# Folding the tokens of the Fourier group ahead of the DFT, and its channel products in three products of parts

## The chip, the core and the metric

The kernel runs on one core of a Trainium2 chip. The metric is the time of one execution on the device, in microseconds; lower is better. TensorE (PE in the profile) multiplies and writes to PSUM, VectorE (DVE), ScalarE (ACT) and GpSimd (POOL) do the elementwise work, and DMAs are issued by SyncE (SP), ScalarE and GpSimd.

## The reference

One layer of an encoder block on 256 tokens of width 2048, in float32: a normalised input is projected to q, k, v and u; twelve attention heads work on q, k, v; a Fourier group of four channel groups of 128 works on u; both results are normalised, joined, projected and added to x; a gated feed-forward part and a last normalisation follow. The part that changes is the Fourier group:

```python
def _fourier_mix(u, w_fourier):
    B, S = u.shape[0], u.shape[1]
    ug = u.reshape(B, S, N_FOURIER_GROUPS, FOURIER_GROUP_DIM).astype(jnp.float32)
    f = jnp.real(jnp.fft.fft2(ug, axes=(1, 3), norm='ortho'))
    y = jnp.einsum('bsgc,gcd->bsgd', f.astype(u.dtype), w_fourier)
    return y.reshape(B, S, FOURIER_WIDTH)
```

The real part of the two-dimensional DFT is cos over positions times cos over channels, less sin over positions times sin over channels. Position k and position 256-k have the same cosine and opposite sines, so the kernel computes the products for 129 cosines and 127 sines only and joins them into 256 positions at the end.

## The kernel before

Products of float32 matrices are done by parts: each operand is split into a high part, rounded to the matmul's reduced float32 (F32R), and a low part, the rest; high x high, low x high and high x low are summed in PSUM. The weights come in *units* of 1 MB (`raw`, three buffers). ScalarE rounds a unit to its high part, VectorE subtracts to get the low part, two units ahead of the multiplication; when the low part is done, the load of the unit three further on is issued on SyncE's queue.

The order is written by hand. `unit(i, work)` runs what was posted under `before` for unit i, then the unit's matmuls, then what was posted `beside` it, then the split of unit i+2, then what was posted `behind` it. Every engine takes its instructions in that order, so a step's place sets both its due time and what queues behind it. Units 0 to 3 give u (in PSUM tiles `ps_u`), 4 to 7 give v (`ps_v`), 8 to 23 the k and q heads, 24 to 39 the output projection; then come the feed-forward items. The numbers of raw tiles are unit numbers: raw7 is the weights of unit 7.

The Fourier group is done in steps posted between these units:

- `rows_out` (L462): u, scaled by each token's 1/rms (`r1`, from GpSimd), leaves PSUM as `u_hi` (L466, ScalarE) and `u_lo` (L467, VectorE), beside unit 5; both blocks of 128 tokens.
- `fourier_positions` (L529): the constant `pos` (cosines and sines of the positions, two blocks of 128 tokens x 256 columns) is split into `pos_hi` and `pos_lo`, beside unit 5.
- `fourier_weights` (L540) before unit 6: the channel DFT is multiplied into `w_fourier`, giving `ps_g` for cosine and sine; `fourier_weights_out` (L550) copies them to `Gs` in plain float32.
- `fourier_rows` (L559) before unit 7: for each of four groups six F32R matmuls (two token blocks x three products), with u as the weights and 256 columns of `pos` moving, into `ps_f`. `fourier_rows_out` (L571) copies the result to `uf` in plain float32, alternately on ScalarE and VectorE.
- `fourier_channels` (L582), before units 8, 9, 10 and 11, one group each: two plain F32 matmuls, 129 columns of cosine and 127 of sine, into `ps_y`. `fourier_channels_copy` brings the result to SBUF, `fourier_channels_join` adds and subtracts to get the 256 positions, `fourier_channels_out` squares and splits it for the output projection.

`row_by_hbm` (L318), behind unit 4, writes the token scales `r1` to HBM as a row by a GpSimd DMA, and reads them back over all partitions (`r1b`) for the keys.

PSUM tiles come from two pools of four banks: `mm` holds u, v, k, q; `dn` holds the Fourier and attention products.

Of the kernel before, what the change touches and what calls it, by code (L numbers as in the profile page):

```python
# [13 lines left out]
P = 128  # L14
D = 2048
S = 256
# [13 lines left out]
WARM = 7  # L30

U_HEAD, U_ROW = 16, 768


SHIFT = 16
# [83 lines left out]
def block_kernel(  # L119
# [30 lines left out]
    def bank(pool, name):  # L150
        return pool.tile([P, 512], F32, tag=pool.name, name=name)
# [66 lines left out]
    vec = base.tile([P, 232], F32, tag="vec", name="vec")  # L218
    chan = cat_pool.tile([P, 512], F32, tag="cat", name="chan")[:, 0 : 2 * P]
    wfs = cat_pool.tile([P, FW], F32, tag="cat", name="wfs")  # L220
    pos = cat_pool.tile([P, 2, S], F32, tag="cat", name="pos")
    Gs = [cat_pool.tile([P, FW], F32, tag="cat", name=f"G{c}") for c in range(2)]
    pos_hi = cat_pool.tile([P, 2, S], F32R, tag="cat", name="pos_hi")
    pos_lo = cat_pool.tile([P, 2, S], F32R, tag="cat", name="pos_lo")
    chan_parts = cat_pool.tile([P, 2, 2 * P], F32R, tag="cat", name="chan_parts")
    wfs_parts = [cat_pool.tile([P, FW], F32R, tag="cat", name=f"wfs_{p}") for p in ("hi", "lo")]
    rel = cat_pool.tile([P, 512], F32, tag="cat", name="rel")
# [156 lines left out]
    def at(when, i, f, *a):  # L384
        when.setdefault(i, []).append((f, a))
# [85 lines left out]
    def row_parts(name):  # L471
        return [
            ph.tile([P, 2, FW], F32R, tag=f"{name}_{p}", name=f"{name}_{p}")
            for p in ("hi", "lo")
        ]

    u_hi, u_lo = row_parts("u")
    v_hi, v_lo = row_parts("v")
    r1b = ph.tile([P, S], F32, tag="r1b", name="r1b")
    for c in range(2, 4):  # L480
        at(beside, 4, token_sums, c)
    at(beside, 4, lambda: fourier_parts())
    at(beside, 4, token_scales)
    at(beside, 5, rows_out, u_hi, u_lo, ps_u)
    at(behind, 5, query_scales)

    cat = {}

# [60 lines left out]

    def fourier_weights_out():  # L550
        for part in range(2):
            nc.scalar.activation(Gs[part], held.pop(("g", part)), AF.Copy)

    H = S // 2
    us = []

    def fourier_rows():  # L559
        for g in range(NG):  # L560
            ps = held["f", g] = bank(dn, f"ps_f{g}")
            for b in range(2):
                for n, (u, w) in enumerate(
                    [(u_hi, pos_hi), (u_hi, pos_lo), (u_lo, pos_hi)]
                ):
                    nc.tensor.matmul(
                        ps[:, 0:S], u[:, b, g * P : (g + 1) * P], w[:, b, :],
                        start=b == 0 and n == 0, stop=b == 1 and n == 2,
                    )

    def fourier_rows_out():  # L571
        for g in range(NG):
            t = ph.tile([P, 512], F32, tag="sc", name=f"uf{g}", bufs=4)[:, 0:S]
            if g % 2:
                nc.scalar.activation(t, held.pop(("f", g))[:, 0:S], AF.Copy)
            else:
                nc.vector.tensor_copy(t, held.pop(("f", g))[:, 0:S])
            us.append(t)

    sq_f = ph.tile([P, S], F32, tag="sqf", name="sq_f")  # L580

    def fourier_channels(g):  # L582
        ps = held["y", g] = bank(dn, f"ps_y{g}")
        for part, o, n in ((0, 0, H + 1), (1, H + 1, H - 1)):
            nc.tensor.matmul(
                ps[:, o : o + n], Gs[part][:, g * P : (g + 1) * P],
                us[g][:, o : o + n], start=True, stop=True,
            )


    def fourier_channels_copy(g):
        h = held["h", g] = ph.tile([P, S], F32, tag="tmp", name=f"yh{g}", bufs=2)
        nc.scalar.activation(h, held.pop(("y", g))[:, 0:S], AF.Copy)

    def fourier_channels_join(g):
        h = held.pop(("h", g))
        y = held["y", g] = ph.tile([P, S], F32, tag="add", name=f"y{g}", bufs=2)
        nc.vector.tensor_tensor(y[:, 1:H], h[:, 1:H], h[:, H + 1 : S], ALU.add)
        nc.vector.tensor_tensor(
            y[:, H + 1 : S], h[:, H - 1 : 0 : -1], h[:, S - 1 : H : -1], ALU.subtract  # L600
        )
        nc.vector.tensor_copy(y[:, 0 : H + 1 : H], h[:, 0 : H + 1 : H])

    def fourier_channels_out(g):
        feature_out(held.pop(("y", g)), NH + g, vcol(V_GF + g), sq_f, g == 0)
# [12 lines left out]
    at(before, 6, fourier_weights)  # L618
    at(beside, 6, fourier_weights_out)
    at(behind, 4, row_by_hbm, r1, r1b, "1")  # L620
    at(before, 7, fourier_rows)
    at(beside, 7, fourier_rows_out)
    at(beside, 8, lambda: rows_out(v_hi, v_lo, ps_v))
    at(behind, 8, distances)

    def fourier_channels_steps():
        for g in range(NG):
            i = 8 + g
            at(before, i, fourier_channels, g)
            at(beside, i, fourier_channels_copy, g)  # L630
            at(behind, i, fourier_channels_join, g)
            at(beside, i + 1, fourier_channels_out, g)
        at(behind, N_OUT + 1, total_scale, sq_f, "f", FW)
# [752 lines left out]
def _layout(inp):  # L1386

    import numpy as np

    f = lambda a: np.ascontiguousarray(np.asarray(a), dtype=np.float32)  # L1390
    x = f(inp["x"]).reshape(2, P, D)

    def tiles(v):
        return f(v).reshape(-1, P).T

    def moving(w, cols):

# [24 lines left out]
    w_up = np.asarray(inp["w_up"])  # L1422
    wup = np.concatenate(
        [still(w_up, o + j * P) for j in range(NF) for o in (0, DFF)]
    )
    w_dn = np.asarray(inp["w_down"])
    def rows_by(tiles, cols):

        w = f(w_dn[tiles[0] * P : (tiles[-1] + 1) * P, cols : cols + 512])
        return w.reshape(len(tiles), P, 512).transpose(1, 0, 2).reshape(P, -1)  # L1430

    downs = [
        rows_by(range(k, k + m), c + n)
        for first, m in GROUPS
        for c in (0, 512)
        for k in (first, first + m)
        for n in (0, 1024)
    ]
    late = [rows_by(LATE, 512 * c) for c in range(4)]
    dw = f(inp["dw_w"]).reshape(3, NF, P).transpose(2, 1, 0).reshape(P, 3 * NF)  # L1440
    sink = np.broadcast_to(f(inp["sink"])[None, :], (P, NH))
    vecs = np.concatenate(
        [tiles(inp["norm2_g"]), tiles(inp["attn_out_g"]),
         tiles(inp["fourier_out_g"]), dw, tiles(inp["dw_b"]), sink], axis=1,
    )
    t = np.arange(S)
    ang = 2.0 * np.pi * ((t[:, None] * t[None, :]) % S) / S
    c_pos = np.concatenate(
        [np.cos(ang[:, : S // 2 + 1]), np.sin(ang[:, 1 : S // 2])], axis=1
    )  # L1450
    c_pos = c_pos.reshape(2, P, S).transpose(1, 0, 2)
    k = np.arange(P)
    ang = 2.0 * np.pi * ((k[:, None] * k[None, :]) % P) / P
    c_chan = np.concatenate([np.cos(ang), -np.sin(ang)], axis=1) / np.sqrt(S * P)
    dist = np.abs(t[:, None] - t[None, :]).astype(np.float64)
    c_rel = np.where(dist <= WINDOW, dist, FAR).reshape(2, P, S).transpose(1, 0, 2)
    return {
        "x": np.ascontiguousarray(x.transpose(1, 0, 2)),
        "w_u_x": np.ascontiguousarray(u_x),
        "vecs": np.ascontiguousarray(vecs),  # L1460
        "wf": np.ascontiguousarray(f(inp["w_fourier"]).transpose(1, 0, 2).reshape(P, FW)),
        "w_in": win,
        "w_out": wout,
        "w_up": wup,
        "w_down_two": np.stack(downs[:8]),
        "w_down": np.stack(downs[8:]),
        "w_down_late": np.stack(late),
        "w_down_last": np.stack([rows_by(LAST, 512 * c) for c in range(4)]),
        "normf_g": f(inp["normf_g"]),
        "c_pos": np.ascontiguousarray(c_pos, dtype=np.float32),  # L1470
        "c_chan": np.ascontiguousarray(c_chan, dtype=np.float32),
        "c_rel": np.ascontiguousarray(c_rel.reshape(P, 2 * S), dtype=np.float32),
    }
# [16 lines left out]
```

## Time and profile before

| | |
|---|---|
| median of 3 runs | 934.08 us (933.99 to 934.61) |
| the profiled execution | 934.68 us |
| its span, first to last instruction | 932.9 us |
| granted TensorE clock | 0.997 |
| PE, VectorE, ScalarE busy | 99%, 83%, 58% |
| position DFT `ps_f`, 24 matmuls | 45.21 to 48.09 us in the chain |
| channel products `ps_y`, four times | 53.52, 59.43, 65.35 and 71.97 us |

The views used are: the page (busy times and the chain of work that ended last), the chain in order of time (start, length, matmul), the timeline of one engine (start, length, engine, line, operation, out<-in, and in brackets the idle time before it and what ended it), the rows of one tile, DMA issues with their time to landing, and the stretches (busy time of each engine in a stretch, granted clock, DMA share and GB/s). A matmul's own duration in a timeline includes its pipeline; its price in a stream is the distance to the next one, which the chain shows. An instruction `LDWEIGHTS` (PEld) is the load of a matmul's weights.

### The profile page before, as it was taken

How to read it: one execution, taken by the hardware profiler on the slowest of the kernel's cores; microseconds unless marked ns; L12 is line 12 of the kernel's file. 1: busy time of each engine (PE TensorE's matmuls, PEld its weight loads, DVE VectorE, ACT ScalarE, POOL GpSimd, SP SyncE). 2: the span in 40 equal slices, each digit the busy share in tenths (PEclk: the TensorE clock that was granted, in tenths of full speed). 3: DMA queues.
4: the chain of work that ended last, by engine and by line, in shares of the span. 5: the costliest groups of instructions: out<-in, count | busy, mean ns of one | idle time of the engine just before them, and what ended most of it. 6: DMA issues, size and time to landing. Idle time of an engine off the chain costs nothing.

```text
span 932.9 us, 12860 instructions
## 1 busy us (share of the span) xinstructions
PE 924.0 (99%) x4981; PEld 800.8 (86%) x4981; DVE 772.4 (83%) x988; ACT 542.3 (58%) x675; POOL 63.0 (7%) x80
## 2 busy tenths in 40 slices
PE   9999999999999999999999999999999999999996
PEld 7888998888888888888888888888888888888885
DVE  7668988787768877898878997888979789989995
ACT  7756776546455655566555665555755556655553
POOL 0101111200000000000000000000000000000002
PEclk9999999999999999999999999999999999999998
DMA  9965877657778668788798779887787968779652
GB/s 365 316 216 169 248 237 209 209 180 276 229 264 275 201 200 261 242 276 261 230 288 256 239 212 299 224 261 234 264 243 241 309 221 271 238 234 272 204 180 91
DMA packets 59309, 224.96 MB, mean 241 GB/s; under 512 B 24400, under 2 KB 29904, under 8 KB 35696
## 3 DMA queue, kind: packets, MB, share of 16 engines
q1 hardware_dynamic: 54560, 194.39, 58.3%
q0 software_dynamic: 4544, 29.49, 17.1%
q8 instruction: 39, 0.64, 0.3%
q10 hardware_dynamic: 144, 0.26, 0.1%
q14 instruction: 22, 0.18, 0.1%
HBM read 217.04 MB, written 7.08 MB: 240 GB/s over the span
## 4 chain that ended last, share of the span: by engine, by line
PE 98%; DMA 0%; ACT 0%; DVE 0%; issue 0%; POOLq 0%; POOL 0%; ACTq 0%
PE ps_val L364 25%; PE ps_gate L364 25%; PE ps_q L364 7%; PE ps_P L1161 3%; PE ps_P L1160 3%; PE ps_P L1162 3%; PE ps_N L1160 3%; PE ps_N L1161 3%; PE ps_N L1162 3%; PE ps_a L347 2%; PE ps_k L364 2%; PE ps_a L349 2%; PE ps_a L348 2%; PE ps_s L676 1%; PE ps_o L770 1%; PE ps_ff L347 1%
## 5 line engine op out<-in xcount | busy, mean ns | idle before, releaser
L203 DVE TENSOR_TENSOR lo<-raw,hi 128x2048 fp32r<-128x2048 f32 (+2 forms) x133 | 294.9, 2220 | 31.9 <-ACT hi L195 31.5
L195 ACT ACTIVATE hi<-raw 128x2048 fp32r<-128x2048 f32 (+1 forms) x131 | 246.8, 1886 | 28.2 <-PE ps_a L348 10.2
L364 PE MATMUL ps_gate<-hU,hi 128*128 128x512 f32 x688 | 236.2, 389 | 0.0
L364 PE MATMUL ps_val<-hU,hi 128*128 128x512 f32 x688 | 236.2, 389 | 0.0
L364 PE MATMUL ps_gate<-hU,lo 128*128 128x256 f32 x688 | 190.0, 276 | 0.0
L364 PE MATMUL ps_val<-hU,lo 128*128 128x256 f32 x687 | 189.7, 276 | 0.0
L364 PEld LDWEIGHTS ps_val<-hU,hi 128*128 128x128 f32 x688 | 129.2, 188 | 26.9
L364 PEld LDWEIGHTS ps_gate<-hU,hi 128*128 128x128 f32 x688 | 129.1, 188 | 26.8
L364 PEld LDWEIGHTS ps_gate<-hU,lo 128*128 128x128 f32 x688 | 129.2, 188 | 1.3
L364 PEld LDWEIGHTS ps_val<-hU,lo 128*128 128x128 f32 x687 | 129.0, 188 | 1.3
L941 ACT ACTIVATE ft_g<-ps_gate 128x256 f32<-128x256 f32 x43 | 16.5, 384 | 120.6 <-PE ps_gate L364 120.6
L941 ACT ACTIVATE ft_v<-ps_val 128x256 f32<-128x256 f32 x43 | 16.4, 383 | 86.7 <-PE ps_val L364 86.7
L364 PE MATMUL ps_q<-hT,hi 128*128 128x512 f32 x192 | 65.0, 391 | 0.0
L1160 PE MATMUL ps_P<-hi_P,op_P 128*128 128x512 f32 x144 | 56.1, 389 | 0.0
L1161 PE MATMUL ps_P<-hi_P,op_P 128*128 128x512 f32 x144 | 56.0, 389 | 0.0
L1162 PE MATMUL ps_P<-lo_P,op_P 128*128 128x512 f32 x144 | 56.0, 389 | 0.0
L364 PE MATMUL ps_q<-hT,lo 128*128 128x256 f32 x192 | 51.3, 277 | 0.0
L1058 DVE TENSOR_TENSOR lo_N<-sumw,hi_N 128x2048 fp32r<-128x2048 f32 (+1 forms) x20 | 41.5, 2076 | 9.4 <-ACT hi_N L1057 9.2
L1160 PE MATMUL ps_N<-hi_N,op_N 128*128 128x512 f32 x108 | 42.0, 389 | 0.0
L1161 PE MATMUL ps_N<-hi_N,op_N 128*128 128x512 f32 x108 | 42.0, 389 | 0.0
L1162 PE MATMUL ps_N<-lo_N,op_N 128*128 128x512 f32 x108 | 42.0, 389 | 0.0
L364 PEld LDWEIGHTS ps_q<-hT,hi 128*128 128x128 f32 x192 | 35.2, 188 | 6.6
(402 smaller groups left out, 1588.8 us busy)
## 6 DMA issues: line engine op xcount, KB each, us to landing
raw<-in_w_up SPq DMA_DIRECT2D x86, 1024.0 KB, 6.8
raw<-in_w_in SPq DMA_DIRECT2D x20, 1024.0 KB, 7.2
raw<-in_w_out SPq DMA_DIRECT2D x16, 1024.0 KB, 5.0
sumw<-in_w_down POOLq DMA_DIRECT2D x16, 1024.0 KB, 8.6
raw<-in_w_down_late SPq DMA_DIRECT2D x4, 1024.0 KB, 6.9
raw<-in_w_down_last SPq DMA_DIRECT2D x4, 768.0 KB, 4.3
turnp<-flip SPq DMA_DIRECT2D x44, 64.0 KB, 1.9
flop<-turnp SPq DMA_DIRECT2D x11, 256.0 KB, 3.2
```

Source lines behind the costliest of these rows:

```text
L195: nc.scalar.activation(halves[i][0][:, s], raws[i][:, s], AF.Copy)
L203: nc.vector.tensor_tensor(lo[:, s], raws[i][:, s], f32(hi[:, s]), ALU.subtract)
L347: nc.tensor.matmul(ps, ah, wh, start=first and q == q0, stop=False)
L348: nc.tensor.matmul(ps, al, wh, start=False, stop=False)
L349: nc.tensor.matmul(ps, ah, wl, start=False, stop=last and q == q0 + len(kk) - 1)
L364: nc.tensor.matmul(ps[:, x], (hi, lo)[i][:, k * P : (k + 1) * P], hk(k)[:, x], start=n == 0 and k == 0, stop=n == len(order) - 1 and k == ...
L676: nc.tensor.matmul(ps[:, b * S : (b + 1) * S], qT[:, qo + b * P : qo + (b + 1) * P], kT[:, ko : ko + S], start=n == 0, stop=n == 2,)
L941: nc.scalar.activation(tmp, ps[:, S : 2 * S], AF.Copy)
L1058: nc.vector.tensor_tensor(lo, src, f32(hi), ALU.subtract)
L1160: nc.tensor.matmul(ps, o[:, 0, p, :], hi[:, s], start=first and p == 0, stop=False)
L1161: nc.tensor.matmul(ps, o[:, 1, p, :], hi[:, s], start=False, stop=False)
L1162: nc.tensor.matmul(ps, o[:, 0, p, :], lo[:, s], start=False, stop=last and p == n - 1)
```

## The change

Tokens t and 256-t, for t from 1 to 127, have the same cosine and opposite sines, so their sum and their difference are formed once and the DFT over positions runs over 128 rows instead of 256. Token 0 stays as it is; token 128 is put beside it, in row 0, and the constants of row 0 are set to fit.

- `fold_turned`, `fold_back`, `fold` and `fold_low` take the place of `rows_out` for u. Tokens 128 to 255 are scaled to SBUF on ScalarE and turned by two VectorE transposes, the second of which reads reversed, so that the 32 rows of each quadrant stand in reverse order. Five DMAs on ScalarE's queue put the quadrants in reverse order at the partitions 1 to 127 and token 128 at partition 0. VectorE forms sum and difference with tokens 0 to 127, ScalarE rounds them, VectorE takes the low parts.
- `fourier_rows` now runs before unit 8. For each group three products with the difference and three with the sum, of 260, 130, 194 and three times 130 columns: sines at columns 0 to 129 of the PSUM tile, cosines at 130 to 259.
- `fourier_rows_out` splits the result into F32R parts (`uf_hi`, `uf_lo`), and `fourier_weights_out` splits `Gs` likewise. `fourier_channels`, before units 9 to 12, is three products of parts for sine and three for cosine, 130 columns each.
- `fourier_channels_copy` copies the sine half only; `fourier_channels_join` reads the cosine half from PSUM. The cosines stand with odd positions first, then even ones.
- The constant `pos` has 402 columns instead of 512.

```diff
     u_hi, u_lo = row_parts("u")
+    folded = {}
+
+    def fold_turned():
+        t, w = (ph.tile([P, 512], F32, tag="sc", name=f"u_{n}", bufs=4) for n in ("1", "turned"))
+        nc.scalar.activation(t, ps_u[1], AF.Copy, scale=r1[:, 1:2])
+        nc.vector.transpose(w, t)
+        w = w.rearrange("p (f i) -> p f i", i=32)[:, :, ::-1]
+        nc.vector.transpose(t.rearrange("p (f i) -> p f i", i=32), w)
+        folded["turned"] = t
+
+    def fold_back():
+        t = folded.pop("turned")
+        back = folded["back"] = ph.tile([P, 512], F32, tag="sc", name="u_back", bufs=4)
+        for q in range(3, -1, -1):
+            n, p = 32 - (q == 0), 97 - 32 * q
+            nc.scalar.dma_start(back[p : p + n], t[32 * q : 32 * q + n])
+        nc.scalar.dma_start(back[0:1], t[31:32])
+
+    def fold():
+        back = folded.pop("back")
+        for q, op in enumerate((ALU.add, ALU.subtract)):
+            t = ph.tile([P, 512], F32, tag="sc", name=f"u_fold{q}", bufs=4)
+            nc.vector.scalar_tensor_tensor(t, ps_u[0], r1[:, 0:1], back, ALU.mult, op)
+            nc.scalar.activation(u_hi[:, q, :], t, AF.Copy)
+            folded[q] = t
+
+    def fold_low():
+        for q in range(2):
+            nc.vector.tensor_tensor(u_lo[:, q, :], folded.pop(q), f32(u_hi[:, q, :]), ALU.subtract)
...
-    at(beside, 5, rows_out, u_hi, u_lo, ps_u)
+    at(beside, 5, fold_turned)
     at(behind, 5, query_scales)
+    at(behind, 5, fold_back)
+    at(behind, 6, fold)
+    at(behind, 6, fold_low)
...
-            nc.scalar.activation(Gs[part], held.pop(("g", part)), AF.Copy)
+            ps, (hi, lo) = held.pop(("g", part)), Gs[part]
+            nc.scalar.activation(hi, ps, AF.Copy)
+            nc.vector.tensor_tensor(lo, ps, f32(hi), ALU.subtract)
...
+    def fourier_rows(g):
+        ps = held["f", g] = bank(dn, f"ps_f{g}")
+        c = slice(g * P, (g + 1) * P)
+        odd_sin, cos = N_SIN + H // 2, slice(POS_S, N_POS)
+        for n, (u, w, q, src, o) in enumerate([
+            (u_hi, pos_hi, 1, slice(0, 2 * N_SIN), 0),
+            (u_hi, pos_lo, 1, slice(0, N_SIN), 0),
+            (u_lo, pos_hi, 1, slice(0, odd_sin), 0),
+            (u_hi, pos_hi, 0, cos, N_SIN),
+            (u_hi, pos_lo, 0, cos, N_SIN),
+            (u_lo, pos_hi, 0, cos, N_SIN),
+        ]):
+            nc.tensor.matmul(
+                ps[:, o : o + src.stop - src.start], u[:, q, c], w[:, src],
+                start=n == 0, stop=n == 5,
+            )
+
+    def fourier_rows_out(g):
+        ps = held.pop(("f", g))[:, 0 : 2 * N_SIN].rearrange("p (a k) -> p a k", a=2)
+        hi = ph.tile([P, 512], F32R, tag="sc", name=f"uf_hi{g}", bufs=4)
+        lo = ph.tile([P, 512], F32R, tag=f"pt{g % 2}", name=f"uf_lo{g}", bufs=2)
...
+        nc.scalar.activation(hi, ps, AF.Copy)
+        nc.vector.tensor_tensor(lo, ps, f32(hi), ALU.subtract)
...
-        for part, o, n in ((0, 0, H + 1), (1, H + 1, H - 1)):
-            nc.tensor.matmul(
-                ps[:, o : o + n], Gs[part][:, g * P : (g + 1) * P],
-                us[g][:, o : o + n], start=True, stop=True,
-            )
+        for part, o, u in ((1, 0, 0), (0, N_SIN, U_COS)):
+            for n, (w, x) in enumerate([(0, 0), (0, 1), (1, 0)]):
+                nc.tensor.matmul(
+                    ps[:, o : o + N_SIN], Gs[part][w][:, g * P : (g + 1) * P],
+                    us[g][x][:, u : u + N_SIN], start=n == 0, stop=n == 2,
+                )
...
-    at(before, 7, fourier_rows)
-    at(beside, 7, fourier_rows_out)
     at(beside, 8, lambda: rows_out(v_hi, v_lo, ps_v))
+    for g in range(NG):
+        at(before, 8, fourier_rows, g)
+        at(beside, 8 + g // 2, fourier_rows_out, g)
     at(behind, 8, distances)
...
-            i = 8 + g
+            i = 9 + g
```

(`H` is 128, `N_SIN` 130, `POS_S` 272, `N_POS` 402, `U_COS` 144.)

More of the change, by code (lines that the diff above doesn't have):

```diff
@@ L32 @@
 U_HEAD, U_ROW = 16, 768
+H = S // 2
+N_SIN = H + 2
+POS_S, N_POS = 272, 272 + N_SIN
+U_COS = 144
 SHIFT = 16
@@ L220, in block_kernel @@
     wfs = cat_pool.tile([P, FW], F32, tag="cat", name="wfs")
[L221 to L224, printed above, removed]
+    pos = cat_pool.tile([P, 512], F32, tag="cat", name="pos")[:, 0:N_POS]
+    Gs = [
+        [cat_pool.tile([P, FW], F32R, tag="cat", name=f"G{c}_{p}") for p in ("hi", "lo")]
+        for c in range(2)
+    ]
+    pos_hi, pos_lo = (
+        cat_pool.tile([P, 512], F32R, tag="cat", name=f"pos_{p}")[:, 0:N_POS]
+        for p in ("hi", "lo")
+    )
     chan_parts = cat_pool.tile([P, 2, 2 * P], F32R, tag="cat", name="chan_parts")
@@ L551, in fourier_weights_out @@
         for part in range(2):
[L552 to L568, printed above, removed]
-                    )
@@ L571, in fourier_rows_out @@
[L571 to L578, printed above, removed]
+            ps, (hi, lo) = held.pop(("g", part)), Gs[part]
+            nc.scalar.activation(hi, ps, AF.Copy)
+            nc.vector.tensor_tensor(lo, ps, f32(hi), ALU.subtract)
@@ new lines, in block_kernel @@
+    us = {}
+    def fourier_rows(g):
[14 more added lines that the diff above has]
+            )
@@ new lines, in fourier_rows_out @@
+    def fourier_rows_out(g):
+        ps = held.pop(("f", g))[:, 0 : 2 * N_SIN].rearrange("p (a k) -> p a k", a=2)
+        hi = ph.tile([P, 512], F32R, tag="sc", name=f"uf_hi{g}", bufs=4)
+        lo = ph.tile([P, 512], F32R, tag=f"pt{g % 2}", name=f"uf_lo{g}", bufs=2)
+        us[g] = hi, lo
+        hi, lo = (
+            t[:, 0 : 2 * U_COS].rearrange("p (a k) -> p a k", a=2)[:, :, 0:N_SIN]
+            for t in (hi, lo)
+        )
+        nc.scalar.activation(hi, ps, AF.Copy)
+        nc.vector.tensor_tensor(lo, ps, f32(hi), ALU.subtract)
@@ L583, in fourier_channels, with odd_even @@
         ps = held["y", g] = bank(dn, f"ps_y{g}")
-        for part, o, n in ((0, 0, H + 1), (1, H + 1, H - 1)):
-            nc.tensor.matmul(
-                ps[:, o : o + n], Gs[part][:, g * P : (g + 1) * P],
-                us[g][:, o : o + n], start=True, stop=True,
-            )
+        for part, o, u in ((1, 0, 0), (0, N_SIN, U_COS)):
[3 more added lines that the diff above has]
+                    us[g][x][:, u : u + N_SIN], start=n == 0, stop=n == 2,
+                )
     def fourier_channels_copy(g):
         h = held["h", g] = ph.tile([P, S], F32, tag="tmp", name=f"yh{g}", bufs=2)
-        nc.scalar.activation(h, held.pop(("y", g))[:, 0:S], AF.Copy)
+        nc.scalar.activation(h[:, 0:N_SIN], held["y", g][:, 0:N_SIN], AF.Copy)
     def fourier_channels_join(g):
-        h = held.pop(("h", g))
+        h, ps = held.pop(("h", g)), held.pop(("y", g))
         y = held["y", g] = ph.tile([P, S], F32, tag="add", name=f"y{g}", bufs=2)
-        nc.vector.tensor_tensor(y[:, 1:H], h[:, 1:H], h[:, H + 1 : S], ALU.add)
+        def odd_even(t):
+            return t.rearrange("p (m e) -> p e m", e=2)
+        cos = ps[:, N_SIN : N_SIN + H].rearrange("p (e m) -> p e m", e=2)
         nc.vector.tensor_tensor(
-            y[:, H + 1 : S], h[:, H - 1 : 0 : -1], h[:, S - 1 : H : -1], ALU.subtract
+            odd_even(y[:, 0:H])[:, ::-1, :], cos, odd_even(h[:, 0:H])[:, ::-1, :], ALU.add
         )
-        nc.vector.tensor_copy(y[:, 0 : H + 1 : H], h[:, 0 : H + 1 : H])
+        cos = ps[:, N_SIN : N_SIN + H + 2].rearrange("p (e m) -> p e m", e=2)[:, :, 0 : H // 2]
+        nc.vector.tensor_tensor(
+            odd_even(y[:, S - 1 : H - 1 : -1]), cos, odd_even(h[:, 1 : H + 1]), ALU.subtract
+        )
     def fourier_channels_out(g):
@@ L1447, in _layout @@
     ang = 2.0 * np.pi * ((t[:, None] * t[None, :]) % S) / S
[L1448 to L1451, printed above, removed]
+    near, k = ang[:H], np.r_[np.arange(1, H, 2), np.arange(0, H + 1, 2)]
+    even = (k % 2 == 0) * 1.0
+    c_pos = np.zeros((P, N_POS))
+    c_pos[1:, 1:H] = np.sin(near[1:, 1:H])
+    c_pos[0, N_SIN : N_SIN + H + 1] = 1.0 - even
+    c_pos[:, POS_S : POS_S + H + 1] = np.cos(near[:, k])
+    c_pos[0, POS_S : POS_S + H + 1] = even
     k = np.arange(P)
```

## The prediction

> **What bounds the kernel now.** I read the page's busy times and chain first, then the chain in order of time around the Fourier group, then the weight loads there, and last what ScalarE, VectorE and the DMA do in the same ten microseconds.
>
> ```profile
> span 932.9 us, 12860 instructions
> PE 924.0 (99%) x4981; PEld 800.8 (86%) x4981; DVE 772.4 (83%) x988; ACT 542.3 (58%) x675; POOL 63.0 (7%) x80
> PE 98%; DMA 0%; ACT 0%; DVE 0%; issue 0%; POOLq 0%; POOL 0%; ACTq 0%
> ```
>
> TensorE is busy 99% of the span and is 98% of the chain that ends last. So the price of an edit is what it does to the row of matmuls, plus any hole that it tears into it; work on other engines is free while it makes no hole.
>
> ```profile
> 38.35 1.37 PE ps_g L545 x6
> ...
> 45.21 2.88 PE ps_f L566 x24
> 48.09 0.23 PE ps_v L347
> ...
> 53.52 0.44 PE ps_y L585 x4
> 53.97 5.47 PE ps_k L364 x32
> 59.43 0.44 PE ps_y L585 x4
> 59.88 0.81 PE ps_q L364 x4
> ```
>
> This is the chain (start, length). The position DFT ps_f is 24 F32R matmuls of 256 columns in 2.88 us, 0.120 each. The channel products ps_y stand four times on it with 0.44: two F32 matmuls of 129 and 127 columns, each run as two passes, so 0.11 a pass. Together 2.88 + 4 x 0.44 = 4.64 us: all that the change can win.
>
> ```profile
> 59.16 0.53 PEld L585 LDWEIGHTS ps_y<-uf,G 128*128 128x128 f32 x4
> 59.61 0.30 PEld L364 LDWEIGHTS ps_q<-hT,hi 128*128 128x128 f32 x2
> ```
>
> Four weight loads begin between 59.16 and 59.61, one per 0.1125 us, as far apart as the passes of ps_y. Narrow passes go at the beat of the loads.
>
> **The matmuls.** Both stages change. Position DFT: per group six matmuls of 256 columns become 260, 130, 194, 130, 130, 130. Channel products: per group two F32 matmuls (four passes) become six F32R matmuls of 130. Instead of 24 + 16 = 40 passes there are 24 + 24 = 48, each with its own load of 128 columns of weights. No F32R matmul below 256 columns is in the trace, so its price is bounded:
> - From below by the stream. Six matmuls of 512 in ps_g take 1.37, 0.228 each; against 0.120 at 256 that is 0.00042 us a column, which gives 0.067 at 130, 0.094 at 194, 0.122 at 260. Then 4 x (0.122 + 0.094 + 4 x 0.067) = 1.93 and 24 x 0.067 = 1.60: 3.53, or 1.1 us won.
> - By the load: 0.11 (ps_y) to 0.12 (ps_f, where load and stream are nearly equal). 48 x 0.115 = 5.52, or 0.9 us lost (0.64 to 1.12).
> - From above by what F32 costs at this width: 0.22 for 128 columns, so 0.223 at 130 and 0.333 at 194. Then 4 x (0.12 + 0.333 + 4 x 0.223) + 24 x 0.223 = 10.7, or 6.1 us lost.
>
> I take the load, +0.9 us: the row of loads 0.1125 apart is the nearest one to a 130-column pass. The cut in columns then wins nothing, and the eight more passes cost.
>
> **The fold.** Before, u goes from PSUM to two parts in ScalarE and VectorE. Now tokens 128 to 255 are scaled, reversed by two VectorE transposes, moved across partitions by five DMAs on ScalarE's queue, folded twice on VectorE, rounded on ScalarE and subtracted on VectorE. For this the position DFT moves from ahead of unit 7 to ahead of unit 8. Unit 7's 24 matmuls of ps_v (0.23 each, 5.46 in all) then follow unit 6 directly at 45.21, and ps_f is due at 45.21 + 5.46 = 50.67. Its first matmul needs the high part of the difference, its third the low part.
>
> ```profile
> 38.36 1.27 ACT L466 ACTIVATE u_hi<-ps_u,rstd 128x512 fp32r<-128x512 f32 x2 [3.26 <-POOL rstd L307]
> 39.51 0.63 ACT L530 ACTIVATE pos_hi<-pos 128x512 fp32r<-128x512 f32 x1
> 40.03 1.91 ACT L195 ACTIVATE hi<-raw 128x2048 fp32r<-128x2048 f32 x1
> 41.84 1.07 ACT L552 ACTIVATE G<-ps_g 128x512 f32<-128x512 f32 x2
> 42.79 1.93 ACT L195 ACTIVATE hi<-raw 128x2048 fp32r<-128x2048 f32 x1
> ```
> ```profile
> 928.32 0.37 ACTq L1223 DMA_DIRECT2D out_y<-z_P  x1
> ```
> ```profile
> 39.08 1.41 DVE L467 SCALAR_TENSOR_TENSOR u_lo<-ps_u,rstd,u_hi 128x512 fp32r<-128x512 f32 x2 [1.32 <-ACT u_hi L466]
> 40.41 0.68 DVE L531 TENSOR_TENSOR pos_lo<-pos,pos_hi 128x512 fp32r<-128x512 f32 x1
> 41.98 2.29 DVE L203 TENSOR_TENSOR lo<-raw,hi 128x2048 fp32r<-128x2048 f32 x1 [0.90 <-ACT hi L195]
> ...
> 44.75 2.29 DVE L203 TENSOR_TENSOR lo<-raw,hi 128x2048 fp32r<-128x2048 f32 x1
> ...
> 50.75 2.29 DVE L203 TENSOR_TENSOR lo<-raw,hi 128x2048 fp32r<-128x2048 f32 x1 [2.92 <-ACT hi L195]
> ```
> ```profile
> L328 DVE STREAM_TRANSPOSE flip<-sc x11: 711/711/712, 81.9 to 164.0; 128x512 f32<-128x512 f32 x11
> ```
>
> In the new order, ScalarE: scaling 38.4 to 39.0, pos_hi to 39.5, raw7's high part to 41.4, five issues at 0.37 to 43.2 (one issue row, far away, but of that queue), G's two to 44.3, raw8's high part to 46.2. VectorE: two transposes of 0.71 to 40.5, pos_lo, raw7's low part to 43.7, three tiny scales to 44.2, two G_lo (0.68 each, as pos_lo) to 45.5, raw8's low part 46.2 to 48.5. So the fold cannot begin before 48.5. Call L the time when it does. Two folds (0.7 each), the second rounding (0.7) and the second low part (0.7) end at L + 2.9; two matmuls of 0.12 run before that part is needed. The hole ahead of ps_f is L + 2.9 - 0.24 - 50.67 = L - 48.0: half a microsecond at best. Unit 7's own parts are there by 43.7, ahead of 45.21.
>
> What sets L beyond 48.5 is the landing of the five copies, issued from 41.4 to 43.2.
>
> The issue of the row of token scales on GpSimd; the landing times (last number) of what was issued between 37 and 39; of the flips of the scores; and the stretches around:
>
> ```profile
> 38.64 0.93 POOL L321 DMA_DIRECT2D row<-rstd  x1 [0.32 <-POOL rstd L307]
> ```
> ```profile
> raw<-in_w_in SPq DMA_DIRECT2D x1, 1024.0 KB, 10.9
> row<-rstd POOLq DMA_DIRECT2D x1, 1.0 KB, 11.1
> ```
> ```profile
> L331 SPq DMA_DIRECT2D turnp<-flip x44: 302/452/1213, 82.6 to 166.1; - x44
> ...
> DMA to landing us min/median/max: 1.7/2.0/5.4
> ```
> ```profile
> 40.00:42.00 2.00, 2.00 (x10) 1.63 (x9) 1.10 (x3) 2.00 (x3) 0.00 (x0) 1.00 0.93 393
> 42.00:44.00 2.00, 2.00 (x11) 1.65 (x10) 2.00 (x1) 2.00 (x3) 0.00 (x0) 1.00 0.06 17
> 44.00:46.00 2.00, 2.00 (x14) 1.80 (x13) 1.84 (x5) 0.72 (x1) 0.00 (x0) 1.00 1.98 66
> 46.00:48.00 2.00, 2.00 (x19) 2.00 (x18) 1.80 (x3) 0.39 (x1) 0.00 (x0) 1.00 0.09 8
> 48.00:50.00 2.00, 2.00 (x11) 1.65 (x10) 0.00 (x0) 1.58 (x2) 0.00 (x0) 1.00 0.67 41
> 50.00:52.00 2.00, 2.00 (x10) 1.66 (x9) 1.25 (x1) 1.41 (x2) 0.59 (x1) 1.00 0.59 197
> ```
>
> In the stretches (busy time of PE, weight loads, VectorE, ScalarE and GpSimd, then clock, DMA share and GB/s) the DMA falls from 393 to 17, 66, 8 and 41 between 42 and 50. A 1 KB transfer, the row of token scales issued at 38.64, lands after 11.1 us at 49.7. The flips of the scores, the nearest copies out of SBUF, land in 1.7 to 5.4 us when this row is not about; then the copies are there by 48.6 at worst. If they sit behind the row, L is about 49.7, and up to 52 when throughput is back. I take 49.7, because the copies start just as the transfers stop: a hole of 1.7 us.
>
> The Trainium skill ("DMA: Bandwidth & Descriptors", "Issuing engines are not separate DMA queues") says that transfers of the scalar, sync and gpsimd queues end up on the same 16 DMA engines and interleave; by that rule ScalarE's queue is no way round, and the sum is the one with 1.7. The rows shown are of GpSimd's and SyncE's queues alone, so they bear out half of it.
>
> Behind the waiting fold VectorE holds raw9's low part; with L = 49.7 its high part ends about 53.8 and the low part about 56.1, while PE takes it after ps_f and unit 8 (5.47), past 60. SyncE's next load waits for that low part, 3 us later than now (it now starts at 50.75 and ends at 53.0); even at 10.9 us it lands by 67, and it is multiplied as unit 12, past 75. The further splits of the transform (ps_f's four, G's two) and the joins lie in VectorE's gaps, such as 48 to 50 with 0.00 busy; without those they would cost about 0.4 us each. A later channel step leaves the PSUM banks and the due times of scores alone. The smaller constant lands long before its use at 39.5: nothing.
>
> **Sum.** +0.9 and +1.7 make +2.6 us. The profiled execution took 934.68 (span 932.9, 1.8 around it), so 937.3 there; its run lies 0.6 above the median 934.08, and on the median's scale it is 936.7. What a measurement of this kernel can tell from no change is about 0.2%, 1.9 us.
>
> **Rivals.**
> 1. *The copies land early* (flip rows, 2 us): L = 48.5, hole 0.5, sum +1.4, 935.5. For it: SBUF to SBUF touches no row in HBM. Against: the weight transfer issued beside that row, also bound for SBUF, needed 10.9 us.
> 2. *A narrow F32R matmul costs as an F32 one of its width*: +6.1 + 1.7 = +7.8, 941.9. For it: only widths of 256 and 512 are shown at the low price. Against: F32's 0.22 is two passes with two loads, and F32R has one.
> 3. *Narrow matmuls stream* and the load hides: -1.1, with a hole of 0.5 to 1.7 between -0.6 and +0.6, about 934.1: not slower. It decides at the beat: below 4.64 / 48 = 0.097 a matmul the products are a gain. Against it: F32 passes of 128 columns keep 0.11 though the stream's row gives 0.067.
>
> The Trainium skill ("TensorE: Matmul & The Clock Gate", "Back-to-back issue gap") gives the third rival: columns / 2.4 + 2.5 ns for a warm matmul, an estimated 57 ns at 130, by which both stages would take 3.0 us and 1.6 would be won ahead of the hole. The trace's 0.110 and 0.228 us for 128 and 512 columns both lie above that formula.
>
> **Chances.** Forecast 0.42; copies early 0.20; F32's price 0.22; stream 0.13; something else, on the faster side, 0.03. Slower by over 0.2%: 0.42 + 0.22 = 0.64. Within: 0.20 and 0.11 of the stream, 0.31. Faster: 0.02 of the stream with a finer beat and the rest, 0.05. The range from 933.9 to 942.4 drops the lower half of the stream, the upper part of F32's price, and the rest, together under 0.2.
>
> **What would show it.** In the profile after, the chain should have ps_f with 24 matmuls in 2.6 to 2.9 us and ps_y with six in 0.66 to 0.72; 1.3 and 1.3 would be F32's price, 0.48 and 0.40 the stream. Ahead of ps_f PE should stand idle by about 1.7 us, released by u_lo; the fold's wait on VectorE should name the copies, landed near 49.7. If PE has no hole there, the fold's term is wrong; if there are holes at later units, the cover of the raw parts was thinner than I read.

## The result and the profile after

The changed kernel takes 946.04 us (median of 6 runs, 944.47 to 951.02) where the kernel before takes 934.18 (6 runs, 933.99 to 934.99): 1.0133 times as long, 95% interval 1.0110 to 1.0155. That is 11.9 us slower; the prediction said 2.6 slower and a range up to 942.4. The direction was right, the size was not. The profiled execution took 946.27, its span is 944.5, or 11.6 more than before. A few executions, of e6, e8, e9 and of the kernel before, took 1.5% to 2% longer and are left out of the times below; the profiles of e6 and e8 (spans of 954.5) are of this kind, with 5.60 us a unit for 5.44 from some 258 us on, and are read ahead of that only.

The page of the changed kernel: span, busy times, chain by engine, granted clock in 40 slices.

```profile
span 944.5 us, 12894 instructions
PE 929.3 (98%) x4989; PEld 805.0 (85%) x4989; DVE 776.6 (82%) x992; ACT 542.9 (57%) x678; POOL 64.0 (7%) x80
PEclk9979999999999999999999999999999999999998
PE 93%; DMA 4%; DVE 1%; ACT 1%; SPq 0%; POOL 0%; ACTq 0%; issue 0%; POOLq 0%; DVEq 0%
```

TensorE, which was 98% of the chain, is now 93%, and DMA has 4%. The third slice of the clock, 47 to 71 us, is a 7. The chain of the changed kernel in order of time shows both (start, length):

```profile
43.63 11.18 DMA u_back<-u
...
54.94 1.42 DVE u_fold L513 x2
...
56.38 0.64 ACT u_hi L514
...
57.06 0.70 PE ps_f L617 x2
...
57.79 4.98 PE ps_f L617 x22
62.77 6.76 PE ps_k L374 x32
69.52 0.62 PE ps_y L640 x6
70.14 5.51 PE ps_q L374 x32
```

The last of the five copies is issued at 43.6 and lands 11.2 us later. VectorE's fold waits for it until 54.94, and the position DFT `ps_f` for the fold until 57.06. Then `ps_f` takes 5.7 us and the next unit 6.76 where later ones take 5.51. The stretches of the changed kernel (its length, then PE's busy time; the granted clock is the third number from the end) say why:

```profile
50.00:52.00 2.00, 0.91 (x5) 0.41 (x3) 0.00 (x0) 0.00 (x0) 0.59 (x1) 1.00 0.46 135
52.00:54.00 2.00, 0.00 (x0) 0.00 (x0) 0.00 (x0) 0.00 (x0) 0.00 (x0) 1.00 1.01 410
54.00:56.00 2.00, 0.00 (x0) 0.00 (x0) 1.06 (x2) 0.28 (x1) 0.00 (x0) 0.70 1.10 324
56.00:58.00 2.00, 0.91 (x3) 0.72 (x4) 1.70 (x3) 1.97 (x3) 0.00 (x0) 0.50 0.34 135
...
60.00:65.00 5.00, 5.00 (x20) 4.61 (x21) 5.00 (x6) 3.08 (x5) 0.00 (x0) 0.50 0.59 192
65.00:70.00 5.00, 5.00 (x34) 4.47 (x32) 1.82 (x8) 0.38 (x1) 0.00 (x0) 1.00 0.66 228
```

PE is idle from 50.9 to 57.06, 6.2 us. Within that hole the clock falls to half, and it stays there until 65: TensorE comes back to work at half speed. My reading after this profile, before any experiment: the 11.6 us are 6.2 of hole, some 4.3 of half clock (`ps_f` 5.7 against some 2.7, `ps_k` 6.76 against 5.51) and some 0.5 of narrow passes (`ps_y` 4 x (0.62 - 0.44) lost, `ps_f` 0.2 won), 11.0 together; another 0.3 was there ahead of the Fourier steps, where `ps_g` starts at 38.45 for 38.19. The theory to test was that the copies are held up by the row of token scales which GpSimd writes to HBM beside them. Its rivals were that the copies themselves are slow, that the clock is no cause but goes along, and that the narrow passes cost more than they show.

### The profile page after: what moved, and what is told of

It reads as the page before. It is cut to its first block, busy times and chain, and to the rows that moved or that the text cites. A ratio compares the mean times of both kernels' runs of the same rounds, so it can differ in the third digit from the quotient of the medians.

```text
span 944.5 us, 12894 instructions
## 1 busy us (share of the span) xinstructions
PE 929.3 (98%) x4989; PEld 805.0 (85%) x4989; DVE 776.6 (82%) x992; ACT 542.9 (57%) x678; POOL 64.0 (7%) x80
## 4 chain that ended last, share of the span: by engine, by line
PE 93%; DMA 4%; DVE 1%; ACT 1%; SPq 0%; POOL 0%; ACTq 0%; issue 0%; POOLq 0%; DVEq 0%
PE ps_gate L374 25%; PE ps_val L374 25%; PE ps_q L374 7%; PE ps_P L1224 3%; PE ps_P L1225 3%; PE ps_P L1226 3%; PE ps_N L1224 3%; PE ps_N L1225 3%; PE ps_N L1226 3%; PE ps_k L374 2%; PE ps_a L359 2%; PE ps_a L357 2%; PE ps_a L358 2%; DMA chan<-in_c_chan 2%; DMA ux<-in_w_u_x 1%; DMA u_back<-u 1%
```

## The experiments

The kernel before took 934.18 us beside the change and 934.5 to 934.7 beside each of the runs e1 to e11; medians of executions, in us:

| kernel | time | over before |
|---|---|---|
| the change | 946.04 | 11.9 |
| e1: no row | 942.78 | 8.3 |
| e2: no copies | 935.25 | 0.7 |
| e3: the hole filled with matmuls | 942.18 | 7.7 |
| e4: row passes one unit later | 939.34 | 4.8 |
| e5: the 31-row copy in two | 946.02 | 11.5 |
| e6: both e1 and e5 | 941.82 | 7.3 |
| e7: the row after the copies | 942.24 | 7.7 |
| e8: as e7, fold alone | 941.36 | 6.8 |
| e9: nothing waits | 935.63 | 1.0 |
| e10: products of parts alone | 935.30 | 0.6 |
| e11: as e9, fold alone | 934.66 | 0.0 |

### e2: the fold without its five copies

```diff
-        back = folded["back"] = ph.tile([P, 512], F32, tag="sc", name="u_back", bufs=4)
-        for q in range(3, -1, -1):
-            ...
-        nc.scalar.dma_start(back[0:1], t[31:32])
+        folded["back"] = t
```

> The changed kernel without the five copies: the fold takes the turned tokens from the partitions where they are (the move across partitions is left out). Whatever holds the copies, no DMA is waited for. ScalarE is also rid of 4 us of issues, so raw8's low part is done near 46.3 and the fold follows at once: no hole. What is left is the price of the passes: the position DFT 24 x 0.104 to 0.115 instead of 2.88, the channel products 4 x 0.62 to 0.69 instead of 4 x 0.44, together +0.4 to +0.9: 934.6 to 935.1. If narrow F32R matmuls had the price of F32, the position DFT would still be 5 us and the time 940.

935.25, ratio 1.0007 (0.9998 to 1.0017). Its chain around `ps_f`:

```profile
50.53 2.66 PE ps_f L613 x24
53.19 5.52 PE ps_k L374 x32
58.71 0.62 PE ps_y L636 x6
```

Without the copies `ps_f` follows unit 7 directly, the clock is 1.00, and the whole change in matmuls costs what the chain shows: 2.66 for 2.88, and four times 0.62 for 0.44, together +0.5. Everything beyond that hangs on the copies: on waiting for them and, as e6 will show, on the time that ScalarE takes to issue them.

### e10: the three products of parts alone, in the kernel before

```diff
...
-        for part, o, n in ((0, 0, H + 1), (1, H + 1, H - 1)):
-            nc.tensor.matmul(
-                ps[:, o : o + n], Gs[part][:, g * P : (g + 1) * P],
-                us[g][:, o : o + n], start=True, stop=True,
-            )
+        for part, o, u, m in ((0, 0, 0, H + 2), (1, H + 2, H, H)):
+            for n, (w, x) in enumerate([(0, 0), (0, 1), (1, 0)]):
+                nc.tensor.matmul(
+                    ps[:, o : o + m], Gs[part][w][:, g * P : (g + 1) * P],
+                    us[g][x][:, u : u + m], start=n == 0, stop=n == 2,
+                )
...
```

> The kernel before with the three products of parts alone: no fold, no copies; four narrow F32R passes (130 and 128 columns) more per channel group than before's two in F32. By the pitch of 0.103 us seen in the changed kernel: six of them 0.62 against 0.44, four groups, +0.7 us, 935.2 where the kernel before takes 934.5; by the prediction's 0.115 +1.0; if the parts' extra work on VectorE and ScalarE (G's and uf's low parts) makes something wait, more, with a hole ahead of ps_y.

935.30, 0.65 over before, ratio 1.0007 (0.9998 to 1.0015). Its chain has the four groups of channel products at 0.62:

```profile
53.00 0.62 PE ps_y L591 x6
53.62 5.51 PE ps_k L367 x32
59.13 0.62 PE ps_y L591 x6
```

Here nothing waits; the products by parts lose 4 x 0.18 = 0.7, as expected, and no later effect of the extra splits shows.

### e1: no row of token scales

```diff
-    at(behind, 4, row_by_hbm, r1, r1b, "1")
+    at(behind, 4, lambda: nc.gpsimd.memset(r1b, 1.0))
```

> The changed kernel without the row of token scales: the two GpSimd transfers by way of HBM are left out and the keys are multiplied by 1 instead. Theory 'row': the five copies are held behind the row's small writes to HBM; without it they land within 2 to 5 us of their issue, VectorE takes up the fold as soon as raw8's low part is done (49.5 in the changed kernel's trace), the hole ahead of ps_f is 1.0 us instead of 6.2, TensorE's clock stays at 1.0, and the time is about 936. Theory 'weights': the copies are slow because the 1 MB weight loads share the DMA engines; they still land 10 us after their issue, the hole stays near 6, and the time stays near 946.

942.78, ratio 1.0087 (1.0072 to 1.0102): much better than the change, far from the 936 expected. The issue-to-landing times of the copies, in the changed kernel first and then in e1 (min, median, max of the three whose landing is recorded: two of 32 rows and the single row):

```profile
DMA to landing us min/median/max: 9.7/10.0/11.2
```
```profile
DMA to landing us min/median/max: 2.1/2.9/7.1
```

So the row does hold the copies up: without it the 32-row copies land in 2 to 3 us where they took 9.7 to 10.0. (e1 leaves out both its transfers, the write to HBM and the reading back, and does not tell them apart.) But one still takes 7.1, the single row. It is queued behind the copy of 31 rows; and SyncE issues the next 1 MB of weights at 43.62, 0.6 us ahead of it, which lands at 50.0, the single row at 51.3. The fold begins at 51.5 instead of 54.9, PE still has a hole of 3.0 us, and the clock still falls. The row was a cause, and not the only one.

### e5 and e6: the copy of 31 rows as 16 and 15

```diff
-            nc.scalar.dma_start(back[p : p + n], t[32 * q : 32 * q + n])
+            for i, m in [(0, 32)] if n == 32 else [(0, 16), (16, 15)]:
+                nc.scalar.dma_start(back[p + i : p + i + m], t[32 * q + i : 32 * q + i + m])
```

e5 has this edit alone, e6 has it with e1's.

> The changed kernel with the copy of 31 partitions in two, of 16 and of 15. Theory 'two causes': the copies are late for two reasons, each enough for a hole: the row of token scales holds every transfer until about 50, and the copy of 31 partitions goes through one DMA engine, 2 KB at a time between the 8 KB pieces of the weight loads (in the run without the row the copies of 32 landed 2 to 3 us after their issue, and the last, behind the 31, only after 7.1). With the row left as it is, all copies should land by 50 to 52, the hole is 2 to 3.5 us and the clock still falls: 940 to 943. Theory 'row alone': no change, 946. Theory '31 alone': they land in 3 us, hole 1.2, 936.

> The changed kernel with the copy of 31 partitions in two and without the row of token scales (keys multiplied by 1, no transfer by way of HBM). Theory 'two causes': with both gone the copies land 2 to 3 us after their issue, by 47; the fold waits for raw8's low part alone (about 50.5, since a sixth issue on ScalarE's queue puts that part 0.5 later), the hole is 1.5 us, too short for the clock to fall, and the time is 936 to 936.5. If the clock falls already at 1.5 us, 939.

e5: 946.02, ratio 1.0123 (1.0108 to 1.0138), no gain; beside the row the copies land in 8.4 to 10.6 us however they are cut. e6: 941.82, ratio 1.0075 (1.0057 to 1.0093). Its copies land in

```profile
DMA to landing us min/median/max: 2.1/3.1/5.3
```

and its fold, in the timeline of e6's VectorE, no longer waits for them: it starts at 50.2, when the low part of raw8 ends, late because ScalarE issued six copies (0.52 to 1.38 us each) ahead of that unit's high part. The Trainium skill ("DMA: Bandwidth & Descriptors", "Why a DMA increments its semaphore by 16 and not by 1") says that a copy is spread over as many engines, up to 16, as divide its outer dimension: 31 rows go through one engine, 16 rows through sixteen and 15 through fifteen. The longest landing, 7.1 us with 31 rows in one copy and 5.3 with 16 and 15, agrees in direction, and the single row behind them lands after 4.1 where it took 7.1; I had passed over this rule.

What e6 leaves is a hole of 1.35 us ahead of `ps_f` (its first matmul's wait for `u_hi`) and 0.28 more (its third's, for `u_lo`). Even that brought the clock down, as e6's stretches show:

```profile
54.50:55.00 0.50, 0.50 (x7) 0.50 (x6) 0.50 (x1) 0.50 (x2) 0.00 (x0) 0.94 0.13 33
55.00:58.00 3.00, 3.00 (x13) 2.71 (x13) 3.00 (x5) 3.00 (x6) 0.00 (x0) 0.50 0.29 55
58.00:58.50 0.50, 0.50 (x3) 0.42 (x3) 0.50 (x3) 0.15 (x1) 0.00 (x0) 0.64 0.39 147
58.50:60.00 1.50, 1.50 (x11) 1.34 (x10) 1.50 (x1) 0.00 (x0) 0.00 (x0) 1.00 0.99 421
```

Hole 1.6, half of 3.4 us at half clock 1.7, passes 0.5: 3.8; in this execution unit 12 starts 4.75 us later than before (83.34 for 78.59), 0.3 of it already at `ps_g`, so the sum misses some 0.6. The executions in e6's median lost 7.3. Their mean clock was 0.993 to 0.994 where the profiled one has 0.995, so they probably spent longer at half clock; the rest of that difference is open, since no profile of one of them was taken.

### e3: the hole filled

```diff
+    def fill():
+        ps = bank(dn, "ps_fill")
+        for _ in range(27):
+            nc.tensor.matmul(ps, hk(0)[:, 0:P], wfs_parts[0], start=True, stop=True)
+
+    at(before, 8, fill)
     for g in range(NG):
         at(before, 8, fourier_rows, g)
```

> The changed kernel with 27 matmuls of 512 columns (27 x 0.228 = 6.2 us, into a PSUM bank that nobody reads) ahead of the position DFT, where TensorE now stands idle. Theory 'clock': the 6.2 us without a matmul let the granted clock fall to 0.5, and that costs 3.1 us in the position DFT and 1.3 in the unit behind it; with the hole filled the clock stays at 1.0, the position DFT takes 2.5 and the unit 5.5, and the time falls by 4.4 to about 941.7. Theory 'price': narrow F32R matmuls are slow by themselves after a change of stage; the position DFT stays at 5.7 us and the time at 946.

942.18, ratio 1.0081 (1.0066 to 1.0096). The copies are nearly as late as in the change (8.9 to 10.3 us), the stretch of the hole is filled with useless matmuls, and the chain then reads

```profile
57.35 2.69 PE ps_f L617 x22
60.05 5.51 PE ps_k L374 x32
```
```profile
56.00:58.00 2.00, 1.62 (x10) 1.03 (x9) 1.30 (x2) 2.00 (x2) 0.00 (x0) 1.00 0.09 37
```

`ps_f` starts no earlier, but at full clock: 2.69 instead of 4.98, and 5.51 instead of 6.76. Over its own kernel before, e3 loses 7.7 and the change 11.9. So 4.2 us of the loss are the clock, and they go when PE is kept busy.

### e4: the row passes one unit later

```diff
-        at(before, 8, fourier_rows, g)
-        at(beside, 8 + g // 2, fourier_rows_out, g)
+        at(before, 9, fourier_rows, g)
+        at(beside, 9 + g // 2, fourier_rows_out, g)
...
-            i = 9 + g
+            i = 10 + g
```

> The changed kernel with the position DFT one unit later (ahead of unit 9 instead of 8) and the channel products likewise. The copies still land near 54.9; unit 8 fills 5.5 us of the wait. Hole 0.7 us ahead of the position DFT, no drop of the clock; with the passes +0.4 the time is 935.5, within 0.3%. Theory 'price' would leave 5.7 us for the position DFT and 939.

939.34, ratio 1.0050 (1.0033 to 1.0067): a miss. Unit 8 now covers the wait up to 55.5, but in this execution the last copy took 12.0 us:

```profile
43.64 11.98 DMA u_back<-u
...
55.74 0.76 DVE u_fold L513
...
58.59 4.22 PE ps_f L617 x22
62.81 7.21 PE ps_q L374 x32
```

From the landing to the first matmul of `ps_f` the fold needs 2.3 us, and unit 8 ended as the copy landed; PE's waits are 2.3 and 0.3, and this hole, too, cost the clock: 4.22 and 7.21 where full clock gives 2.7 and 5.5. This execution, 941.30, is the slowest of the four; the others took 938.89 to 939.58 at mean clocks of 0.996 to 0.998 for 0.995 here, so the median has less of the clock in it, and how long their holes were is not known.

### e7 and e8: the row after the copies

e7 is e4 with e5's two copies and with the row issued only once the copies have landed; e8 has plain F32 channel products as well, so that the fold is the only part left.

```diff
+    def row_later():
+        seen = ph.tile([P, 2], F32, tag="seen", name="seen")
+        nc.gpsimd.tensor_copy(seen, folded["back"][:, 0:2])
+        row_by_hbm(r1, r1b, "1")
+
+    at(behind, 5, row_later)
...
-    at(behind, 4, row_by_hbm, r1, r1b, "1")
```

> A whole version: copy of 31 partitions in two, the row of token scales issued only once the copies are in (GpSimd reads two columns of them first), and the position DFT and the channel products one unit later. No hole, clock 1.0; what is left of the change is the price of the passes: position DFT 2.66 instead of 2.88, channel products 4 x 0.62 instead of 4 x 0.44, so +0.5: 935.0. If the later row now holds the weight loads of units 10 and 11, there is a hole ahead of those units and 937 or more.

> As the repaired version, but with the channel products as before, two plain F32 matmuls a group, of 130 columns: the fold alone. Position DFT 2.66 instead of 2.88, channel products 4 x 0.44: -0.2, 934.3, no difference that can be measured. If the load of weights were no bound, the fold would be worth 0.9 us and the time 933.6.

942.24 (ratio 1.0082, 1.0069 to 1.0094) and 941.36 (1.0071, 1.0058 to 1.0083): both missed. The hole ahead of `ps_f` is gone, and another has come. e7's chain:

```profile
44.59 4.20 DMA u_back<-u
...
50.39 10.59 DMA row<-rstd
...
61.28 6.42 DMA r1b<-row
...
67.79 0.44 DVE add_k L727
...
70.51 2.29 DVE lo L208
...
74.31 1.69 PE ps_s L746 x6
...
77.17 6.89 PE ps_q L374 x32
```

The row takes 10.6 us even with the copies out of its way, so its length does not come from them; and the copies, issued ahead of it now, land in 2.0 to 5.4. Read back over all partitions it is there at 67.7; VectorE's `add_k`, which multiplies the keys by it, waits for it, and behind that wait stand the low part of a later unit and the q that `ps_s` needs: PE waits 4.0 us (by e7's waits of PE, `ps_s` for `qT`), and the clock falls again. This was the queue behind a waiting instruction that the prediction had looked for behind the fold, and that I overlooked when I moved the row.

### e9 and e11: nothing waits

The row stays at its early place, and everything that hangs on the copies goes later: the first half of u is copied to SBUF so that its PSUM bank comes free, the fold stands behind unit 7, `ps_f` ahead of unit 10, the channel products two units later; the copy of 31 rows is in two. e11 is the same with plain F32 channel products.

```diff
+        folded["u0"] = ph.tile([P, 2, FW], F32, tag="v_lo", name="u_0")[:, 0, :]
+        nc.scalar.activation(folded["u0"], ps_u[0], AF.Copy, scale=r1[:, 0:1])
...
-            nc.vector.scalar_tensor_tensor(t, ps_u[0], r1[:, 0:1], back, ALU.mult, op)
+            nc.vector.tensor_tensor(t, u0, back, op)
...
-    at(behind, 6, fold)
-    at(behind, 6, fold_low)
+    at(behind, 7, fold)
+    at(behind, 7, fold_low)
...
-        at(before, 8, fourier_rows, g)
-        at(beside, 8 + g // 2, fourier_rows_out, g)
+        at(before, 10, fourier_rows, g)
+        at(beside, 10 + g // 2, fourier_rows_out, g)
...
-            i = 9 + g
+            i = 11 + g
```

> The whole change laid out so that nothing should wait for the turned copies: the 31-row copy goes out as 16 and 15 rows, the first half of the Fourier sums is copied to SBUF so that its PSUM bank comes free, the fold stands behind unit 7, the row passes ahead of unit 10 (about 61 us, copies landed at 55.6 at the latest so far), the channel passes two units later. The row of token scales stays where it is. Theory (all of the loss beyond 0.5 us is a hole at ps_f and the clock that falls after it): no hole over 0.5 us between 45 and 90 us, clock 1.00, ps_f 2.7, ps_y 0.62 each, time 0.5 over the kernel before: 935.0 where that is 934.5. Rival (the fold's and the copies' work on VectorE, ScalarE and the queues costs units of its own, wherever the passes stand): a hole of 1 to 3 us remains at unit 9 or 10 and the time stays at 938 or over.

> The layout of e9 with the channel products left in F32 (fold alone). By the traces: ps_f 2.66 against 2.88, ps_y as before: -0.2 us, 934.3 where the kernel before takes 934.5, no more than can be measured; 0.7 under e9.

e9: 935.63, ratio 1.0010 (1.0000 to 1.0019). e11: 934.66, ratio 1.0000 (0.9991 to 1.0009). The copies still land 8 to 10 us after their issue, and no matmul waits for them; e9's copies, a stretch, and the two places of its chain that matter:

```profile
DMA to landing us min/median/max: 7.9/8.9/9.9
```
```profile
55.00:60.00 5.00, 5.00 (x31) 4.41 (x30) 3.96 (x7) 4.47 (x6) 0.00 (x0) 1.00 0.94 390
```
```profile
54.67 0.70 DVE u_fold L516
...
69.60 1.20 PE ps_s L747 x6
70.80 0.62 PE ps_y L643 x6
```

PE has no hole and the clock holds. Of e9's 1.0 us, 0.5 are the passes as in e2; the other 0.5 is in `ps_s` at 69.60, 1.20 long where later ones take 0.72, released, by the chain, by the q that ScalarE and VectorE finish late. In e11 the chain has

```profile
61.43 2.67 PE ps_f L617 x24
```

and `ps_y` at 0.45. By that the fold alone should win 0.2 us, which a time of 934.66 neither shows nor excludes. No version beats the kernel before by more than a measurement can tell.

## Why the prediction was wrong

**The price of the passes: right in kind, a little too high.** I took 48 passes at the beat of the weight load, 0.115, and +0.9 us. In the chain six passes of 130 columns take 0.62, 0.103 each, and the sum is +0.5 (by the medians e2 loses 0.7, and e10, with the products alone, 0.6). The stream's price, 0.067, and F32's, 0.22, are both refuted: `ps_f`, 2.66 in e2, would be 1.93 or 5.4 us. The third rival's turning point, 0.097 a matmul, was near, but on the other side. That the weight load sets the beat is argued from the spacing of the loads; no run changed the load alone. The formula of the Trainium skill ("TensorE: Matmul & The Clock Gate", "Back-to-back issue gap"), by which 1.6 us would have been won, does not hold for these matmuls: an estimated 57 ns where 103 were measured. The same section of the Trainium skill calls it the gap of an isolated matmul and says that it under-counts where a narrow matmul loads its weights; the prediction passed over that.

**The hole: the right formula with the wrong L.** The prediction had hole = L - 48.0, with L the start of the fold. L was 54.94; the formula gives 6.9, and the profile shows 6.2, since the first two matmuls, at half clock, took 0.70 and not 0.24 and so filled the rest of the wait for the low part. The step that failed is "If they sit behind the row, L is about 49.7, and up to 52 when throughput is back". I took the landing of the row as the end of the trouble, and it is not. For the first two copies of 32 rows the step held: issued at 40.3 and 41.3, they landed 9.7 and 10.0 us later, at 50.0 and 51.3, just behind the row, which landed at 49.8. But L waits for the last copy, the single row, issued at 43.6, and that landed at 54.8. Between them, at 43.3, SyncE had issued the next 1 MB of weights, which landed 12.5 us later, at 55.8; the prediction had no such transfer ahead of the last copy. No run issues the last copy ahead of that load, so its part is argued, from the order of landing here and in e1. Counted from its own issue, the last copy was as late as the row and the weight transfer beside it (11.1 and 10.9 in the profile before). A landing time read from a row that is issued into the same trouble should have been added to the copies' own issue time: 43.2 + 10.9 = 54.1. The rows for this were quoted. ScalarE's five issues, put at 0.37 each and done by 43.2, took 0.51 to 1.13, and the last one only began at 43.6, a smaller error.

**The term that was missing: the clock.** The sum had no line for what a hole does to the speed after it. The kernel before hardly lets PE idle, and its page shows the clock falling in the last slice alone, where PE has run out of work:

```profile
PE   9999999999999999999999999999999999999996
PEclk9999999999999999999999999999999999999998
```

The prediction made nothing of that slice, and its range had no bound for such a fall. e3 prices it at 4.2 us, more than a third of the loss.

**Covers.** That the later parts of the weights, the splits of G and `uf` and the joins are covered was right: after 70.14 the changed kernel runs unit by unit as before, and unit 12 starts at 89.97 where it did at 78.59, so that all but 0.2 of the 11.6 us lie before it. Rival 1, copies landing early, came true only where the row was gone or later and the 31-row copy was in two (e6, e7, e8); and even in e6 the hole was 1.6 and not 0.5, because raw8's low part, ahead of the fold on VectorE, ended at 50.2 and not at 48.5.

## What to carry to other kernels

When a step is put behind a transfer, add the landing times of what is issued in the same stretch to the issue time of the transfer's last piece, and place the consumer later than that; here moving the consumer (e9, e11) left no hole, while moving the transfer that held things up (e7) only moved the wait. Where TensorE is 99% busy, as here, a hole cost its length plus half of what ran at half clock after it, and a hole of 1.6 us was enough for that. Cutting 24 matmuls of 256 columns to 130 in four of six won 0.2 of 2.88 us, since a pass went on taking 0.10 to 0.11 us, and each pass added at that width cost about 0.10 us.

## What of the hardware was not expected

**The clock's steps.** The time at half clock comes in equal pieces. In the stretches of the changed kernel around its two edges (granted clock third from the end)

```profile
54.50:55.00 0.50, 0.00 (x0) 0.00 (x0) 0.07 (x1) 0.00 (x0) 0.00 (x0) 0.80 1.22 319
55.00:65.00 10.00, 7.91 (x31) 7.33 (x32) 8.85 (x10) 7.33 (x10) 0.00 (x0) 0.50 0.48 153
65.00:65.50 0.50, 0.50 (x5) 0.45 (x4) 0.50 (x2) 0.00 (x0) 0.00 (x0) 0.96 0.44 180
```

0.80 is a fall at 54.80 and 0.96 a rise at 65.04: 10.24 us. The same reading of e1

```profile
55.00:55.50 0.50, 0.50 (x6) 0.50 (x6) 0.14 (x1) 0.50 (x2) 0.00 (x0) 0.85 0.00 0
...
62.00:62.50 0.50, 0.50 (x4) 0.47 (x4) 0.50 (x4) 0.00 (x0) 0.00 (x0) 0.82 0.00 0
```

gives 55.35 to 62.18, 6.83 us, and of e6 (above) 54.94 to 58.36, 3.42. They are three, two and one times 3.41. The Trainium skill ("TensorE: Matmul & The Clock Gate", "What's actually happening") gives a free-running window of 3.413 us, and these lengths agree. Where the Trainium skill says on the same page that no gap over some 3.4 us should be left ("HAM oscillation — how this bites in real kernels"), the runs ask for less: in e6 waits of 1.35 and 0.28 us brought the clock down, and the fall, at 54.94, came 2.6 us after PE was back at work; in e3 a wait of 0.28 did not. The changed kernel's slowest execution, 951.02 us, had a mean clock of 0.989 against 0.992 in the profiled one, so more of these windows may make up its spread; no profile shows it.

**A 1 KB transfer of 11 us that holds up the others.** The row of token scales takes 11.1 us before, 11.5 in the changed kernel, 11.0 in e9, 9.3 in e4 and 10.6 in e7, where the copies had landed ahead of it; and copies issued within a few microseconds after it land in 8 to 12 us, without it in 2 to 5 (e6). The moving of its bytes does not take that long: in the changed kernel all 32 packets of GpSimd's DMA queue are through by 42.4, the row counts as landed at 49.8, and in between the 16 DMA engines move 55 GB/s in the mean, where they move 284 in the 4 us ahead of that and 258 in the 4 us after. What holds back its landing, and the others with it, was not tried.
